# Both heads of a pair turned by DMA transposes in a two-layer attention kernel

## The chip, the cores and the metric

The kernel runs on one core of one Trainium2 chip. The metric is device time in microseconds of one execution. The median of three runs before the change is 2208.05 us (2207.29 to 2210.84). One further execution was recorded by the hardware profiler.

Engines are named as in the profile: PE is TensorE (matrix multiplication and transposes), DVE is VectorE, ACT is ScalarE, POOL is GpSimd, and SP is the queue that issues all transfers (DMA).

## The reference, cut to what matters

Two layers stand one behind the other. Each computes `x + W_out(attention(RMSNorm(x)) * silu(gate))`, with q, k, v and gate from one combined projection and an RMS norm per head on q and k. There are 2048 prompt rows and 64 sample rows, 1024 features and 16 heads of 64.

- Layer A: 16 query heads share 2 key heads; a query sees its own chunk of 64 rows and the 2 before; each head has a learned sink and a relative bias.
- Layer B: 16 query heads and 16 key heads; a query sees its own chunk and the 8 before; each head has a learned bias by clipped distance. No sinks.

```python
s = jnp.einsum('bqkgd,bskd->bkgqs', qg, k) * (dh ** -0.5) + bias
p = jax.nn.softmax(s, axis=-1)                     # layer B
o = jnp.einsum('bkgqs,bskd->bqkgd', p, v)
y = x + (o * jax.nn.silu(gate)) @ w_out
```

The softmaxed p comes out of the first product with queries on partitions, while the second product needs keys on partitions. So p has to be transposed, tile by tile. This transposition is the subject here.

## The kernel before, in words

**Precision.** Numbers are carried as two halves, a high and a low part. A projection is three matmuls per block of 128 features: high by high, high by low, low by high (L679 to L681). In layer B both halves are fp16, and powers of two (`S_W`, `C_B`, `G_B`) computed from the largest weight of each pair keep them in range.

**Work in layer B.** The 16 heads form 8 pairs (`hp`, 0 to 7). For each pair there are nine units: eight of 256 prompt rows (`u` 0 to 7, two tiles of 128 rows each) and one of the 64 sample rows, which stands between units 6 and 7. A unit is first projected (`gen`, `project`) and later attended.

**Two streams on PE.** PE's order is written out by hand. `pipeline` walks through the attention of the units; between its parts it calls `filler.to(mark)`, which emits as much of the projection work of later units (and, at the end, of the output projection) as a count of PE cost asks for. The other engines' orders come from a scheduler that simulates the program, so an instruction of SP, ACT, DVE or POOL can be placed earlier than it was written.

**A step.** A prompt unit has four steps, in the order (tile 0, head 0), (tile 1, head 0), (tile 0, head 1), (tile 1, head 1); a sample unit has one. A step does `scores`: the score matmuls into a PSUM tile `sb` (two such tiles exist), the biased minimum on DVE (L1420), the exponential on ACT (L1429). Then comes background work, filler, `due(step)` with everything promised for this step, and filler again. After the second step of a unit, `queries` of the next unit transposes q and k on PE into the only `tp` tile (PSUM).

**How p is turned.** `TURNED` lists the heads of a pair that go by DMA, in pairs 1 to 7.

- Head 0 (in `TURNED`): DVE adds log(2^14) to the minimum (L1425), `parts` copies p to fp16 on ACT (L1463) and has POOL subtract for the low half (L1464), both into one of three buffers named `values`; one step later `turn_p` issues the DMA transpose into a `pt` buffer (L1472; there are two). The products (`turned_products`, L1568) follow four steps after the second tile.
- Head 1 (not in `TURNED`): one step later `values` transposes p on PE, block by block, into an `sb` tile (L844), and `split_to` evicts it in two halves by ACT (L816) and DVE (L817). The products (`products`, L1607) follow three steps after the second tile. The transposes of the gates of the unit share the last of these `sb` tiles.
- Pair 0 and the sample unit always go by PE.

Both heads' products add into one PSUM tile `o` (there is one), which `finish` evicts, multiplies by the gates and stores.

**Background work.** `bg` is a list of small jobs: splitting weights (L467, L470), squares and scales of the q and k norms (L756 to L774), gates (L782, L783), low halves of queries (L1367, L1371). `bg.share` takes some from the list. In layer B it is called after every `scores` and after every `values`, so six times in a unit of pairs 1 to 7.

**Weights and the scale chain.** The weights of the next pair are loaded raw (SP, L445) and split into a ring of 12 chunks, 8 of which a pair uses. Four chunks are asked for three filler jobs ahead, the rest one job ahead. Their scale needs a chain: `input_across` (a transpose on PE of one column, L197, then DVE) and `input_scales` (a matmul, L212, then DVE, L213). `scale_work` calls them inside the projection of unit 5. Both use the `tp` tile.

Of the kernel before, what the change touches and what calls it, by code (L numbers as in the profile page):

```python
# [17 lines left out]
P = 128  # L18
# [6 lines left out]
NU = SEQ // UT  # L25
# [9 lines left out]
WB = 3  # L35
XB = 4
XN = 7
EARLY = 3
MORE = 4.7
WN = 12  # L40
AVG_A = 5.02
# [7 lines left out]
QY = 1  # L49
# [1 line left out]
HB, WB_, PB, VB = 2.0 ** 10, 2.0 ** 14, 2.0 ** 14, 16.0  # L51
LAG = 4
HALF = 5 * 2 * P
TURNED = (0,)

@with_exitstack
def hybrid_encoder_kernel(
# [34 lines left out]
    sb = ctx.enter_context(tc.tile_pool(name="sb", bufs=2))  # L92
# [163 lines left out]
    def scale_work(hp, u, e):  # L256
        at = 2 * u + e
        if hp < 7:
            if at < 8:
                scan(8 * (hp + 1) + at)  # L260
            elif at == 8:
                scan()
                input_top(hp + 1)
            elif at == 10:
                input_across(hp + 1)
            elif at == 11:
                input_scales(hp + 1)
            i = 64 + 3 * hp + (at - 11)
            if 11 <= at < 14 and i < 84:
                scan(i)  # L270
            elif at == 14:
                scan()
        elif u == 0:
            (output_top, output_across)[e]()
        elif at == 2:
            output_scales()
# [585 lines left out]
        return Q2[turn[0] % 2]  # L862


    class Filler:
        def __init__(self):
            self.jobs, self.n, self.gen, self.done, self.total = [], -1, None, 0.0, 0.0
            self.attending = False

        def add(self, prefetch, weights, gen, early=True):  # L870
            j = Item()
            j.prefetch, j.weights, j.gen, j.early = prefetch, weights, gen, early
            self.jobs.append(j)

        def step(self):
            if self.gen is None:
                self.n += 1
                if self.n >= len(self.jobs):
                    return False
                if self.n == 0:  # L880
                    self.x = self.jobs[0].prefetch()
                    self.jobs[0].weights()
                for q in self.x.items:
                    bg.run(q)
                if self.n + 1 < len(self.jobs):
                    nxt = self.jobs[self.n + 1]
                    self.x = nxt.prefetch()
                    if nxt.weights is not None:
                        nxt.weights()
                if self.n + EARLY < len(self.jobs):  # L890
                    nxt = self.jobs[self.n + EARLY]
                    if nxt.weights is not None and nxt.early:
                        nxt.weights(WN - 8)
                self.gen = self.jobs[self.n].gen()
# [16 lines left out]
    def layer_a():  # L911
# [4 lines left out]
        def add_unit(qd, place, unit):  # L916
# [117 lines left out]
                mine[0].mark = filler.total  # L1034
            if qd == 0 and unit is order[-1]:
                mine[0].mark += 8 * 3 * 256 / 2400
            filler.add(prefetch, weights if place == 0 else None, first if qd == 0 and u == 0 else gen, qd > 1)

        for qd in range(4):
            for place, unit in enumerate(order[2:5] + order[:2] + order[5:] if qd == 1 else order):  # L1040
# [215 lines left out]
    def layer_b():  # L1256
# [4 lines left out]
        def add_unit(hp, unit):  # L1261
# [14 lines left out]
                return x  # L1276

            def weights(*m):
                if hp not in st.emit:
                    (st.w[hp],), _, st.emit[hp] = load_weights(1, (w_in_b[hp], 512), scale=gsb[:, hp])  # L1280
                st.emit[hp](*m)
# [39 lines left out]

            filler.total += 8 * (6 if T == UT else 2) * 512 / 2400
            it.mark = filler.total
            filler.add(prefetch, weights if u == 0 else None, gen)

        for hp in range(8):
            for unit in order:
# [148 lines left out]
        def values(it, i, h, short):  # L1476
            u, T, tiles = it.unit
            tt, t0, n = tiles[i]
            if i == 0:
                it.ph[h], it.pl[h] = (  # L1480
                    t(x, [P, 5, 256], 2, F32R if u == NU else F16) for x in ("ph", "pl")
                )
            if u == NU:
                n, m, kb = P, 3, 0
            else:
                kt0 = max(tt - 4, 0)
                m, kb = tt - kt0 + 1, kt0 - it.base
            PT = psum_b("sb", 1024, 2)
            PTv = PT.rearrange("p (c x) -> p c x", x=P)
            gates_too = u != NU and it.hp > 0 and (i, h) == (1, 1)  # L1490
            for c in range(m):
                transpose(PTv[:, (kb + c) % 5, :n], it.p[i, h][:n, c * P : (c + 1) * P])
                if short:
                    short.pop(0)()
            while short:
                short.pop(0)()
            if gates_too:
                GT = PT[:, 5 * P : 5 * P + T]
                for e, (_, g0, _) in enumerate(tiles):
                    transpose(GT[:, g0 : g0 + n], it.G[:n, e * P : (e + 1) * P])  # L1500
            bg.anchor(*split_to(
                it.ph[h][:, :m, t0 : t0 + n], it.pl[h][:, :m, t0 : t0 + n], PTv[:, :m, :n],
                None if u == NU else PB,
            ))
            if gates_too:
                it.gt = gate_t(GT.rearrange("p (j s) -> p j s", j=1), T, G_B(it.hp))

        def then(it, i, h):
            late = it.hp > 0 and len(TURNED)
# [66 lines left out]
        def gates(it):  # L1576
            u, T, tiles = it.unit
            n = tiles[0][2]
            GT = psum("tp", 512, 1)
            for e, (_, t0, _) in enumerate(tiles):  # L1580
                transpose(GT[:, t0 : t0 + n], it.G[:n, e * P : (e + 1) * P])
            it.gt = gate_t(GT[:, :T].rearrange("p (j s) -> p j s", j=1), T, G_B(it.hp))
# [12 lines left out]
        def products(it, h):  # L1595
# [17 lines left out]
                product(short[0], 0)  # L1613

            def rest():
                if h == 1 and it.hp == 0:
                    gates(it)
                for y, x in enumerate(full):
                    if y:
                        product(x, 0)  # L1620
                    product(x, 1, stop=y == last)
                if h == 1:
                    finish(it)
# [11 lines left out]
        def pipeline():  # L1635
# [12 lines left out]
            def due(at):  # L1648
                flush()
                now = [x for x in todo if x[0] <= at]  # L1650
                todo[:] = [x for x in todo if x[0] > at]
                short, rests, vals = [], [], []
                for _, kind, x in now:
                    if kind == "products":
                        between, rest = products(*x)
                        short += between
                        rests.append(rest)
                    else:
                        {"values": vals, "call": rests}[kind].append(x)
                for x in vals:  # L1660
                    values(*x, short)
                    bg.share(BL, BP_, KC)
                for fn in short + rests:
                    fn()

            for x, it in enumerate(its):
# [13 lines left out]
                for y, (i, h) in enumerate(heads):  # L1680
# [6 lines left out]
                    if sample and x + 1 < len(its):  # L1687
                        queries(its[x + 1])
                        flush()
                        near = 1e9  # L1690
                    goal(2 * y + 2)
                    if not sample and y == QY and x + 1 < len(its):
                        queries(its[x + 1])
                        near = 1e9
# [234 lines left out]
```

## Time and profile before

| What | Value |
|---|---|
| median of three runs | 2208.05 us |
| profiled execution | 2212.35 us |
| its span | 2210.5 us |
| mean granted PE clock | 0.987 |
| PE, DVE, ACT, POOL busy | 95%, 70%, 64%, 45% of the span |
| DMA queue of SP | 58.0% of 16 engines' time |

In rows of groups, the last two numbers before the bar are the busy time in us and the mean duration of one in ns; after the bar stands the idle time of the engine just before them, and what ended it. A PE duration includes the latency of its pipeline, so it is longer than the distance to the next one. In rows of waits stand the total in us, how often, and the longest. In rows of the timeline stand start and duration in us. In rows of windows stand the stretch, its length, the busy time of PE, PEld (weight loads), DVE, ACT and POOL with the number of instructions in brackets, the granted PE clock, the DMA engines' busy share and GB/s. In the view of one line stand the shortest, median and longest duration in ns.

### The profile page before, as it was taken

What the parts mean: (1) busy time and instruction counts of PE and PEld (TensorE: products, weight loads), DVE (VectorE), ACT (ScalarE), POOL (GpSimd) and SP (SyncE); (2) the same over time, 40 slices, a digit from 0 to 9 for tenths busy, and PEclk for the clock granted to TensorE, in tenths of its full rate; (3) what the DMA queues carried; (4) which work ended last, traced back from release to release, by engine and by line L of the source; (5) the groups of instructions that cost most, each with busy time, mean ns of one, the idle gap of its engine ahead of it and who ended that gap; (6) DMA issues with size and microseconds to landing.
All of it is one profiled execution on the core that took longest, in us unless ns stands there. A gap on an engine that the chain in (4) does not pass through costs nothing.

```text
span 2210.5 us, 41329 instructions
## 1 busy us (share of the span) xinstructions
PE 2110.9 (95%) x13441; PEld 1526.6 (69%) x13441; DVE 1547.2 (70%) x4105; ACT 1424.8 (64%) x3610; POOL 999.5 (45%) x1509
## 2 busy tenths in 40 slices
PE   7999999999999999999999989999999999998999
PEld 6877888787889997555555555555555555566888
DVE  6769777677676456787777776777767767577542
ACT  6878878677785333666666766766667667576420
POOL 5645544334355355853444444444444445443000
PEclk9999999999999999999999999999999999999999
DMA  8856546856545667445465565664646556345664
GB/s 276 275 160 215 180 125 220 229 164 182 180 128 178 216 192 256 158 143 172 117 180 136 128 178 133 160 167 115 196 118 162 158 118 171 95 105 136 198 202 124
DMA packets 383096, 372.87 MB, mean 169 GB/s; under 512 B 174672, under 2 KB 320352, under 8 KB 382848
## 3 DMA queue, kind: packets, MB, share of 16 engines
q1 hardware_dynamic: 382880, 370.23, 58.0%
q8 instruction: 106, 1.74, 0.3%
q14 instruction: 110, 0.90, 0.1%
HBM read 257.59 MB, written 73.43 MB: 150 GB/s over the span
## 4 chain that ended last, share of the span: by engine, by line
PE 58%; DVE 15%; DMA 9%; ACT 8%; issue 6%; POOL 4%; SPq 1%; POOLq 0%; ACTq 0%; DVEq 0%
PE pj L679 9%; PE pj L681 9%; PE pj L680 9%; PE pj L1772 4%; PE pj L1774 4%; PE pj L1773 4%; DMA scan<-in_w_in_b_dram 3%; DVE p L1420 3%; PE sb L844 2%; PE sa L844 2%; PE o L1607 2%; PE tp L844 2%; PE o L1568 2%; PE sb L1416 1%; ACT p L1429 1%
## 5 line engine op out<-in xcount | busy, mean ns | idle before, releaser
L679 PE MATMUL pj<-wh,xx 128*128 128x512 f16 (+2 forms) x1648 | 644.6, 391 | 5.2 <-ACT pb L702 3.9
L681 PE MATMUL pj<-wh,xx 128*128 128x512 f16 (+2 forms) x1648 | 626.4, 380 | 2.5 <-POOL xx L564 2.5
L680 PE MATMUL pj<-wh,xx 128*128 128x512 f16 x1024 | 392.0, 383 | 0.0
L1429 ACT ACTIVATE p<-p,nm 128x640 f32<-128x640 f32 (+5 forms) x264 | 199.2, 754 | 202.6 <-DVE nm L1420 102.4
L1772 PE MATMUL pj<-xx,wh 128*128 128x264 f32 (+1 forms) x1024 | 291.4, 285 | 8.0 <-DVE res L1778 2.7
L1773 PE MATMUL pj<-xx,wh 128*128 128x264 f32 (+1 forms) x1024 | 288.8, 282 | 0.0
L680 PE MATMUL pj<-wl,xx 128*128 128x512 f32 (+1 forms) x624 | 234.1, 375 | 2.2 <-DVE wl L470 2.2
L1420 DVE CUSTOM_DVE_ANT_0 p<-sb,BT 128x640 f32<-128x640 f32 (+5 forms) x272 | 195.7, 720 | 44.7 <-PE sb L1417 42.3
L564 POOL TENSOR_TENSOR xx<-xraw,xx 128x528 fp32r<-128x528 f32 (+4 forms) x144 | 183.8, 1295 | 88.9 <-ACT xx L563 82.1
L1464 POOL TENSOR_TENSOR values<-p,values 128x640 f16<-128x640 f32 (+2 forms) x112 | 141.2, 1261 | 159.4 <-ACT values L1463 158.8
L1250 POOL TENSOR_TENSOR o<-gt,o 128x256 f32<-128x256 f32 (+1 forms) x132 | 100.8, 763 | 207.7 <-DVE o L1249 96.8
L761 POOL TENSOR_TENSOR f<-f,mhalf 128x4 f32<-128x4 f32 (+2 forms) x187 | 187.5, 1003 | 13.7
L681 PEld LDWEIGHTS <-xx 128*128 128x128 f16 x1024 | 101.0, 99 | 126.4 <-issue 4.7
L756 POOL TENSOR_TENSOR sq<-pa 128x256 f32<-128x256 f32 (+2 forms) x187 | 113.1, 605 | 147.1 <-ACT pa L715 94.3
L1156 ACT ACTIVATE p<-p,nm 128x257 f32<-128x257 f32 (+2 forms) x272 | 134.3, 497 | 51.1 <-DVE nm L1150 42.9
L774 DVE TENSOR_TENSOR pa<-pa,f 128x256 f32<-128x256 f32 (+3 forms) x221 | 120.3, 544 | 57.9 <-POOL f L761 53.2
L679 PEld LDWEIGHTS <-xx 128*128 128x128 f16 x1024 | 101.3, 99 | 71.9 <-issue 3.1
L680 PEld LDWEIGHTS <-xx 128*128 128x128 f16 x1024 | 101.1, 99 | 70.1 <-issue 3.0
L1774 PE MATMUL pj<-xx,wl 128*128 128x264 f32 x512 | 145.7, 285 | 0.8 <-DVE wl L463 0.8
L1774 PE MATMUL pj<-xx,wh 128*128 128x264 f16 x512 | 142.7, 279 | 2.1 <-DVE wh L460 2.1
L1150 DVE CUSTOM_DVE_ANT_0 p<-sa,BT,nsink 128x256 f32<-128x256 f32 (+2 forms) x272 | 117.4, 467 | 36.0 <-PE sa L844 29.9
L679 PEld LDWEIGHTS pj<-wh,xx 128*128 128x128 f32 x624 | 118.7, 190 | 23.0 <-ACT pb L702 4.8
(273 smaller groups left out, 5276.9 us busy)
## 6 DMA issues: line engine op xcount, KB each, us to landing
xx<-xsb SPq DMA_DIRECT2D x112, 512.0 KB, 4.1
xx<-xsa SPq DMA_DIRECT2D x88, 512.0 KB, 4.8
xraw<-oga SPq DMA_DIRECT2D x64, 264.0 KB, 3.6
xraw<-ogb SPq DMA_DIRECT2D x64, 264.0 KB, 3.7
xsa<-xx SPq DMA_DIRECT2D x32, 512.0 KB, 4.1
scan<-in_w_in_b_dram SPq DMA_DIRECT2D x64, 256.0 KB, 4.5
wl<-in_w_in_b_dram SPq DMA_DIRECT2D x64, 256.0 KB, 4.1
xraw<-in_x_dram SPq DMA_DIRECT2D x40, 256.0 KB, 4.0
```

Of the source, the lines that this page charges most:

```text
L564: nc.gpsimd.tensor_tensor(lo, rv, wide(hi), op=ALU.subtract)
L679: nc.tensor.matmul(ps[:n, :C], xh, wh, start=k == 0, stop=False)
L680: nc.tensor.matmul(ps[:n, :C], xh, wl, start=False, stop=False)
L681: nc.tensor.matmul(ps[:n, :C], xl, wh, start=False, stop=k == KC - 1)
L761: nc.gpsimd.tensor_tensor(fv, fv, mhalf[:n, :H], op=ALU.pow)
L1156: ex = nc.scalar.activation(pv[:n, h % 2, : nk + 1], pv[:n, h % 2, : nk + 1], AF.Exp, scale=-1.0, bias=nm[:n, h : h + 1], accum_out=sm[:n, ...
L1420: mi = nc.vector.tensor_tensor_reduce(out=p[r, :nk], in0=S[r, o : o + nk], in1=b, op0=ALU.add, op1=ALU.min, scale=1.0, scalar=3e38, accum_ ...
L1429: ex = nc.scalar.activation(p[:n, :nk], p[:n, :nk], AF.Exp, scale=-1.0, bias=it.nm[:n, c : c + 1], accum_out=it.sm[:n, c : c + 1],)
L1464: lo = nc.gpsimd.tensor_tensor(two[:, :, 1, :], pv, two[:, :, 0, :], op=ALU.subtract)
L1772: nc.tensor.matmul(ps[:, :OT], wh, oh, start=k == 0, stop=False)
L1773: nc.tensor.matmul(ps[:, :OT], wh, ol, start=False, stop=False)
L1774: nc.tensor.matmul(ps[:, :OT], wl, oh, start=False, stop=k == KC - 1)
```

## The change

- `TURNED` becomes `(0, 1)`: head 1 of pairs 1 to 7 goes through `parts`, `turn_p` and `turned_products` like head 0. Its products follow four steps after the second tile, and the sample's products and output one step later than before. The multiplication of the reciprocal sums (L1440) falls away, as both heads now carry the same factor, and a factor in `input_across` answers for it.
- `gates` of pairs 1 to 7 takes an `sb` tile of its own, at the time of head 1's products.
- `bg.share` in `due` is called at every step but the first, whether there are `values` or not: eight times a unit.
- `scale_work` puts the two links of the scale chain on a list; `pipeline` takes one link off after the last filler of a prompt unit's fourth step; `weights` of layer B takes what is still there. The second link is put there one tile later than it was called before.
- Four chunks of the next pair's weights are asked for two filler jobs ahead in layer B (`early` is 2), not three. Elsewhere this stays as it was.

```diff
-TURNED = (0,)
+TURNED = (0, 1)
...
             elif at == 10:
-                input_across(hp + 1)
-            elif at == 11:
-                input_scales(hp + 1)
+                held["chain"].append(lambda: input_across(hp + 1))
+            elif at == 12:
+                held["chain"].append(lambda: input_scales(hp + 1))
...
-                if self.n + EARLY < len(self.jobs):
-                    nxt = self.jobs[self.n + EARLY]
-                    if nxt.weights is not None and nxt.early:
+                for nxt in self.jobs[self.n + 2 : self.n + 4]:
+                    if nxt.weights is not None and nxt is self.jobs[min(self.n + nxt.early, len(self.jobs) - 1)]:
                         nxt.weights(WN - 8)
...
             def weights(*m):
+                while held["chain"]:
+                    held["chain"].pop(0)()
...
-            filler.add(prefetch, weights if u == 0 else None, gen)
+            filler.add(prefetch, weights if u == 0 else None, gen, 2)
...
-            gates_too = u != NU and it.hp > 0 and (i, h) == (1, 1)
...
-            if gates_too:
-                GT = PT[:, 5 * P : 5 * P + T]
-                for e, (_, g0, _) in enumerate(tiles):
-                    transpose(GT[:, g0 : g0 + n], it.G[:n, e * P : (e + 1) * P])
...
-            if gates_too:
-                it.gt = gate_t(GT.rearrange("p (j s) -> p j s", j=1), T, G_B(it.hp))
...
-            GT = psum("tp", 512, 1)
+            GT = psum_b("sb", 1024, 2) if it.hp and len(TURNED) else psum("tp", 512, 1)
...
-                if h == 1 and it.hp == 0:
+                if h == 1:
                     gates(it)
...
                 for x in vals:
                     values(*x, short)
+                if at:
                     bg.share(BL, BP_, KC)
...
                     goal(2 * y + 2)
+                    if not sample and y == QY + 2 and held["chain"]:
+                        held["chain"].pop(0)()
```

More of the change, by code (lines that the diff above doesn't have):

```diff
@@ L37 @@
 XN = 7
-EARLY = 3
 MORE = 4.7
@@ L862, in low_queries @@
         return Q2[turn[0] % 2]
+    held["chain"] = []
     class Filler:
@@ L868, in __init__, with add @@
             self.attending = False
-        def add(self, prefetch, weights, gen, early=True):
+        def add(self, prefetch, weights, gen, early=3):
             j = Item()
@@ L1036, in add_unit @@
                 mine[0].mark += 8 * 3 * 256 / 2400
-            filler.add(prefetch, weights if place == 0 else None, first if qd == 0 and u == 0 else gen, qd > 1)
+            filler.add(prefetch, weights if place == 0 else None, first if qd == 0 and u == 0 else gen, 3 * (qd > 1))
         for qd in range(4):
```

## The prediction

> **What bounds the kernel now.** First the page's head, then busy time in windows of one pair of heads (141.2 us is the distance at which the scan loads recur in the chain of work that ended last).
>
> ```profile
> span 2210.5 us, 41329 instructions
> PE 2110.9 (95%) x13441; PEld 1526.6 (69%) x13441; DVE 1547.2 (70%) x4105; ACT 1424.8 (64%) x3610; POOL 999.5 (45%) x1509
> ...
> core 0: us, PE busy (x) PEld busy (x) DVE busy (x) ACT busy (x) POOL busy (x), PEclk, DMA share, GB/s
> 1135.30:1276.50 141.20, 134.28 (x828) 80.07 (x828) 105.33 (x281) 96.08 (x243) 68.10 (x105) 1.00 0.57 149
> 1276.50:1417.70 141.20, 134.04 (x817) 79.73 (x816) 102.41 (x276) 95.34 (x242) 65.57 (x99) 0.99 0.56 149
> ```
>
> In layer B, where the whole change lies, TensorE works 134 of 141 us per pair; VectorE, its nearest rival, 102 to 105. So TensorE's own instructions are the bound, and 7 us a pair are waits. The view of waits of TensorE from 1058 to 2010 us (pairs 1 to 7) says which:
>
> ```profile
> PE sb L844 <- DVE nm L1420: 13.6, 6, 2.7
> PE tp L197 <- DVE KB L1371: 6.7, 6, 3.8
> PE sb L1416 <- DVE nm L1420: 5.6, 6, 1.9
> PE sb L844 <- ACT p L1429: 5.5, 5, 1.4
> PE sb L844 <- DVE pl L817: 3.7, 8, 0.9
> PE sb L1416 <- ACT gt L1237: 2.9, 3, 1.1
> PE sb L844 <- ACT values L719: 2.3, 1, 2.3
> ...
> PE tp L844 <- DVE scl L213: 1.3, 5, 0.3
> ```
>
> 25.1 us (13.6 + 5.5 + 3.7 + 2.3) stand in front of TensorE's transposes of the second head's p, 8.5 us (5.6 + 2.9) in front of score matmuls that share the two `sb` tiles with them, 8.0 us (6.7 + 1.3) at the scale chain. No row names `pt`: the DMA-transposed head is never waited for.
>
> **The change, part by part.**
>
> *Transposes leave TensorE.* A head of one pair has tiles of 1, 2, 3, 4 and twelve times 5 key blocks, 70 in all; seven pairs make 490 instructions. The first row's count agrees: 490, with 140 of pair 0 and 24 of the sample, is 654. The time of one is read from starts in the timeline, since its 0.27 us are latency:
>
> ```profile
> L844 PE MATMUL sb<-ident,p x654: 272/273/422, 899.5 to 2054.2; 128*128 128x128 f32 x164
> ...
> 1478.18 0.71 PE L844 MATMUL sb<-ident,p 128*128 128x128 f32 x5
> 1478.73 0.27 PE L844 MATMUL o<-ident,o 128*64 128x128 f32 x1
> ```
>
> Five take 0.55 us, 0.11 each: 490 x 0.11 = 54 us off the bound. The products stay as many, and the two gate transposes per unit only move to an `sb` tile of their own.
>
> *Waits in front of them.* The 25.1 us lose their instruction, and the score matmuls then find a free `sb` tile two steps back instead of one. But part of this wait is VectorE's debt at the end of a pair. Windows of 5 us and the worst wait there:
>
> ```profile
> 1291.50:1296.50 5.00, 3.41 (x18) 1.76 (x18) 4.70 (x13) 4.46 (x11) 2.07 (x4) 1.00 0.72 173
> 1296.50:1301.50 5.00, 2.33 (x10) 1.48 (x11) 5.00 (x11) 2.58 (x6) 2.66 (x5) 0.81 0.96 348
> ```
>
> VectorE is full there (4.70 and 5.00 of 5), TensorE waits, and its granted clock falls to 0.81. The scores will be late next in that place. Of 25.1 + 8.5 = 33.6 us I take 20 as gone; the ends are 0 and 34.
>
> *Scale chain.* Issued after the last step's filler instead of inside a projection, it finds its `tp` tile free; it can also fall together with the weights, when both links come at once. Of 8.0 us I take 5; ends 8 and -8, a loss as large as now.
>
> *What replaces the transposes.* Per tile, ACT and VectorE no longer split p out of PSUM (L816, L817); instead ACT copies it to fp16, POOL subtracts, SP issues a DMA transpose, and VectorE adds a constant to the minimum (L1425), while one small multiplication a unit (L1440) goes. Groups of pair 3's window, then views of single lines:
>
> ```profile
> L1464 POOL TENSOR_TENSOR values<-p,values 128x640 f16<-128x640 f32 (+4 forms) x16 | 20.0, 1251 | 23.4 <-ACT values L1463 23.3
> L817 DVE SCALAR_TENSOR_TENSOR pl<-sb,ph 128x640 f16<-128x640 f32 (+4 forms) x15 | 11.0, 730 | 2.0 <-ACT ph L816 1.9
> L1463 ACT CAST values<-p 128x640 f16<-128x640 f32 (+4 forms) x16 | 10.5, 653 | 0.2
> L816 ACT ACTIVATE ph<-sb 128x640 f16<-128x640 f32 (+4 forms) x16 | 10.0, 627 | 3.7 <-PE sb L844 3.5
> ...
> L1425 DVE TENSOR_SCALAR nm<-nm x112: 131/145/155, 1057.3 to 2041.1; 128x1 f32<-128x1 f32 x112
> L1440 DVE TENSOR_SCALAR sm<-sm x56: 160/169/259, 1068.7 to 2050.3; 128x2 f32<-128x2 f32 x56
> L1472 SPq DMA_TRANSPOSE pt<-values x112: 1184/1354/2478, 1058.8 to 2044.5; - x112
> DMA to landing us min/median/max: 2.3/3.5/7.5
> ```
>
> Per pair of now about 131 us: VectorE 102 - 16 x 0.73 + 16 x 0.145 - 8 x 0.17 = 92 (70%); ACT 95 - 10.0 + 10.5 = 96 (73%); POOL 66 + 20 = 86 (65%). None becomes the bound; they hide behind TensorE's 124 us. If that cover were gone POOL's 20 us a pair would be 140 us.
>
> *SP and the DMA engines.* 112 more issues of 1.35 us are 22 us a pair on SP's queue. A transfer's share of the engines is bounded by this stretch, which holds one transpose of ten 128x128 blocks and two 32 KB copies:
>
> ```profile
> 1519.52 1.33 SPq L1472 DMA_TRANSPOSE pt<-values  x1
> 1520.95 0.66 SPq L1360 DMA_DIRECT2D q<-q  x1
> ...
> 1520.00:1522.50 2.50, 2.50 (x15) 1.32 (x13) 1.87 (x5) 2.02 (x6) 1.27 (x3) 1.00 0.88 178
> 1522.50:1529.50 7.00, 6.54 (x41) 3.79 (x39) 5.72 (x22) 3.62 (x10) 2.99 (x6) 1.00 0.06 20
> ```
>
> 0.88 x 2.5 = 2.2 us at most, 35 us for 16: 0.56 x 141 = 79 becomes 114 of 131, 0.87. High, yet the next 7 us lie idle at 0.06, so transfers move rather than add up. Cover: from the issue of a head's last transpose to its products are three steps of 131 / 33 = 4.0 us, 12 us against 3.5 (worst 7.5). The ring of three `values` buffers comes round after three steps now, not six: POOL's 1.4 and the landing's 7.5 still fit. The `pt` buffer is freed by products in the step that wants it again, so a transpose can hold SP's queue for a fraction of a step; behind it stand xx loads, q copies and stores. I put nothing for this; ends 0 and 28 (4 us a pair at the full VectorE stretch).
>
> The Trainium skill, VectorE: DVE Perf Modes, section The three transpose paths, speaks against the change: it gives 1309 ns for a 128x128 block by DMA and prefers TensorE where PSUM will do. Ten blocks one by one would be 13.1 us, past the 12 us of cover, by some 1 us a unit, 60 us in all (an estimate from that page). The trace contradicts it: 3.5 us at the median.
>
> *POOL's order.* The query chain of the next unit runs over POOL (L756, L760, L761) and VectorE (L774) to transposes on TensorE. Its slack, in the tightest of six units of one pair, and what a colliding POOL instruction does to a VectorE one:
>
> ```profile
> 1688.47 0.42 DVE L774 TENSOR_TENSOR pa<-pa,f 128x256 f32<-128x256 f32 x1
> 1690.29 0.60 PE L844 MATMUL tp<-ident,pa 128*128 128x128 f32 x4
> ...
> 1498.10 0.91 POOL L1464 TENSOR_TENSOR values<-p,values 128x384 f16<-128x384 f32 x1
> 1498.24 0.93 DVE L783 SCALAR_TENSOR_TENSOR pb<-sq,pb 128x128 f32<-128x128 f32 x1 [0.19 <-ACT sq L782]
> ...
> L783 DVE SCALAR_TENSOR_TENSOR pb<-sq,pb x204: 215/410/1516, 35.4 to 2011.1; 128x128 f32<-128x128 f32 x64, 128x256 f32<-128x256 f32 x32, 128x64 f32<-128x64 f32 x4, 64x256 f32<-64x256 f32 x2
> ```
>
> 1.4 us of slack against one more subtraction of 1.25 us in front: mostly hidden. I take a loss of 5 us over all units; ends 0 and 118 (rival 1).
>
> *Edits with one answer.* The share at every step makes eight a unit instead of six and adds no instruction: 0, between -5 and 5. The first four weight chunks of a pair are split one job later; they run now at 1260 to 1269 us, and the ring lets the other four follow only from 1293:
>
> ```profile
> 1268.78 0.74 DVE L470 SCALAR_TENSOR_TENSOR wh<-wl,gsb,wh 128x512 f16<-128x512 f32 x1
> 1292.91 0.74 DVE L470 SCALAR_TENSOR_TENSOR wh<-wl,gsb,wh 128x512 f16<-128x512 f32 x1
> ```
>
> 24 us of room hide a shift of some 10; without it TensorE would wait four splits, 3 us a pair, 21. The second head's products come one step later, the sample's too; `o` is taken again two steps after that. Costs nothing but one more step at the end, covered by output projections.
>
> The sum: -54 - 20 - 5 + 5 = -74 us. The profiled execution took 2212.35 us (span 2210.5), 4.3 above the median of 2208.05; less 74 from each gives 2138 and 2134.
>
> **The rivals.**
>
> 1. *Slower: the query chain falls behind POOL.* If in each of 56 units two subtractions queue ahead of L760 or L761 (2.8 us) and a VectorE instruction is held 0.7 us more (0.93 against 0.22 for L783), 3.5 less the tightest slack of 1.4 is 2.1 us of wait a unit, 118 us instead of my 5. The sum is then +39: 2247. It decides from 79 / 56 = 1.4 us a unit. For it: rows above; against it: POOL stays idle a third of the time and the two subtractions come a step apart. The Trainium skill, SBUF — State Buffer, section SBUF: two separate sides, calls the port pair of VectorE and POOL an exclusive lock held for a whole instruction; the collision quoted agrees.
>
> 2. *Half given back.* VectorE's debt at the end of each pair and late transfers return the 20 us as score waits and add up to 28: -54 - 5 + 5 + (0 to 28), 2154 to 2182. For it: 5.00 of 5 us and a DMA share of 0.96 in the same window. Against: VectorE gives up 0.73 us a tile there.
>
> 3. *All gained.* All 34 and 8 us go and nothing comes: 2208 - 96 = 2112.
>
> 4. *The change doesn't do what it says.* Waits take up just what leaves, 2208: TensorE would have to be no bound, against 134 of 141 us.
>
> **How the numbers follow.** The forecast (2115 to 2153) 0.55; half back, up to 2203, 0.20; all gained 0.06; no change 0.04; slower 0.15. Within 0.2% (4.4 us) is about what a measurement of this kernel can't tell from no change. Faster 0.81, same 0.04, slower 0.15. The 8-in-10 range, 2105 to 2212, leaves out rival 1 and the lower end.
>
> **What the profile after would show.** Right: 164 or so `sb<-ident,p` transposes on TensorE; 224 DMA transposes; the waits at L844 and L1416 under 14 us; a pair in 130 to 132 us, TensorE 96% busy or more; POOL near 86. Wrong: rows of TensorE waiting at `tp` for L774 (rival 1), at the products for `pt`, at L1416 for L1420 over 30 us (rival 2), or ACT waiting at its copy for the transposes to land.

## The result, and the profile after

The change made the kernel about 1% slower: 2231.57 us (median, 2230.04 to 2233.74) against 2209.45 us (2207.29 to 2212.77) for the kernel before in the runs beside it, a ratio of 1.0095 with a 95% interval of 1.0079 to 1.0111. The forecast of 2134 us and its range, which ended at 2212, were wrong. Lines of the new kernel are numbered a little differently: L774 is now L773, L783 is L782, L470 is L469, L844 is L843; L1416 is now L1418, L1420 is L1422, L1464 is L1466, L1472 is L1474.

The head of the page after, and busy time in the middle 900 us of layer B, first of the kernel after and then of the kernel before:

```profile
span 2228.3 us, 40988 instructions
PE 2078.6 (93%) x12951; PEld 1477.0 (66%) x12951; DVE 1520.2 (68%) x4049; ACT 1436.8 (64%) x3610; POOL 1140.4 (51%) x1621
...
1100.00:2000.00 900.00, 806.72 (x4654) 453.50 (x4652) 617.66 (x1656) 600.49 (x1489) 535.60 (x722) 0.97 0.74 172
```

```profile
1100.00:2000.00 900.00, 860.62 (x5263) 512.37 (x5261) 661.49 (x1763) 613.34 (x1543) 428.75 (x649) 0.99 0.56 145
```

TensorE has 12951 instructions instead of 13441: exactly the 490 transposes are gone. Its busy time fell by 32.3 us (2110.9 to 2078.6), but the time in which it does nothing rose by 50.1 us, from 2210.5 - 2110.9 = 99.6 to 2228.3 - 2078.6 = 149.7. The difference, 17.8 us, is the growth of the span. So this is no story of a dearer instruction on TensorE. In the middle stretch it idles 93 us of 900 where it idled 39. No other engine is full there: VectorE works 618 of 900 us, POOL 536.

TensorE's waits between 1058 and 2040 us (total, times, longest) in the kernel after:

```profile
PE sb L1418 <- DVE nm L1422: 46.9, 26, 3.9
PE sb L1418 <- DMA q<-q: 12.7, 5, 4.3
PE o L843 <- POOL o L1528: 9.1, 6, 1.6
PE o L1521 <- ACT p L1431: 6.6, 5, 1.6
PE tp L196 <- DVE KB L1373: 6.2, 3, 5.5
PE sb L843 <- DVE nm L1422: 5.4, 5, 1.7
PE sb L1418 <- ACT gt L1237: 4.2, 7, 0.7
PE tp L211 <- DVE KB L1373: 4.2, 1, 4.2
```

The waits in front of the transposes went, and a larger one stands in front of the score matmuls. They need an `sb` tile that VectorE frees with its biased minimum (L1422, row `nm`); this cost 5.6 us before and costs 46.9 us now. Nothing waits for `pt`, and no row names `tp` and L773.

Why is VectorE late, when it works less than before? One place in the timeline (start, duration, instruction, in brackets the idle time before it):

```profile
1387.07 1.39 POOL L1466 TENSOR_TENSOR values<-p,values 128x640 f16<-128x640 f32 x1 [0.55 <-ACT values L1465]
1387.13 1.61 DVE L773 TENSOR_TENSOR pa<-pa,f 128x256 f32<-128x256 f32 x1
...
1388.77 0.82 DVE L1422 CUSTOM_DVE_ANT_0 p<-sb,BT 128x640 f32<-128x640 f32 x1
...
1389.66 0.32 PE L1418 MATMUL sb<-KA,q 128*128 128x384 f16 x1 [2.24 <-DVE nm L1422]
```

VectorE's L773 multiplies queries by their scale. It took 0.42 us in the row of the prediction. Here it starts just after a subtraction of POOL and ends just after it, 1.61 us long. The minimum of the softmax is the next instruction in VectorE's order and starts only then; TensorE waits 2.24 us for it, and 1.61 - 0.42 = 1.19 us of that is the stretched instruction. The wait is charged to L1422, which itself was not slow.

Over the whole execution, stretched instructions stand mainly in three groups of VectorE, all reading two inputs from SBUF: the query scales, the gates and the weight splits. Groups of VectorE, first before, then after (last numbers before the bar: busy us, mean ns):

```profile
L774 DVE TENSOR_TENSOR pa<-pa,f 128x256 f32<-128x256 f32 (+3 forms) x221 | 120.3, 544 | 57.9 <-POOL f L761 53.2 <-POOL f L769 2.5
L783 DVE SCALAR_TENSOR_TENSOR pb<-sq,pb 128x128 f32<-128x128 f32 (+3 forms) x204 | 97.7, 479 | 23.3 <-ACT sq L782 22.0
L470 DVE SCALAR_TENSOR_TENSOR wh<-wl,gsb,wh 128x512 f16<-128x512 f32 x64 | 60.0, 942 | 9.9 <-ACT wh L467 9.9
```

```profile
L773 DVE TENSOR_TENSOR pa<-pa,f 128x256 f32<-128x256 f32 (+3 forms) x221 | 150.4, 681 | 46.8 <-POOL f L760 42.2 <-POOL f L768 2.7
L782 DVE SCALAR_TENSOR_TENSOR pb<-sq,pb 128x128 f32<-128x128 f32 (+3 forms) x204 | 106.4, 522 | 40.1 <-ACT sq L781 38.5
L469 DVE SCALAR_TENSOR_TENSOR wh<-wl,gsb,wh 128x512 f16<-128x512 f32 x64 | 65.0, 1022 | 3.9 <-ACT wh L466 3.9
```

The same 489 instructions took 278.0 us before and 321.8 us after, 43.8 more. This sum, most of it ordinary working time, is called the held time below: no shape and no count changed, only what ran beside them. Taken one by one in pairs 1 to 7 (1058 to 2040 us), 96 of them last over 0.15 us longer than the shortest of their shape while a subtraction of POOL that had started first runs beside them: 84 us in all, 42 of it beside head 1's subtractions. In the kernel before it is 41 of them and 36 us.

### The profile page after: what moved, and what is told of

It reads as the page before. It is cut to its first block, busy times and chain, and to the rows that moved or that the text cites. A ratio compares the mean times of both kernels' runs of the same rounds, so it can differ in the third digit from the quotient of the medians.

```text
span 2228.3 us, 40988 instructions
## 1 busy us (share of the span) xinstructions
PE 2078.6 (93%) x12951; PEld 1477.0 (66%) x12951; DVE 1520.2 (68%) x4049; ACT 1436.8 (64%) x3610; POOL 1140.4 (51%) x1621
## 4 chain that ended last, share of the span: by engine, by line
PE 45%; DVE 21%; ACT 9%; DMA 9%; issue 8%; POOL 6%; SPq 1%; ACTq 0%; POOLq 0%; DVEq 0%
PE pj L678 7%; PE pj L680 7%; PE pj L679 7%; PE pj L1770 4%; PE pj L1772 4%; PE pj L1771 4%; DVE p L1422 4%; DVE pa L773 3%; DMA scan<-in_w_in_b_dram 3%; PE sa L843 2%; POOL values L1466 2%; DVE q L1369 2%; DVE o L1249 2%; ACT p L1431 2%; DMA scan<-in_w_o_b_dram 1%
## 5 line engine op out<-in xcount | busy, mean ns | idle before, releaser
L679 PE MATMUL pj<-wh,xx 128*128 128x512 f16 x1024 | 396.7, 387 | 0.9 <-DVE wh L469 0.9
L1466 POOL TENSOR_TENSOR values<-p,values 128x640 f16<-128x640 f32 (+2 forms) x224 | 281.5, 1257 | 133.7 <-ACT values L1465 131.2
L1422 DVE CUSTOM_DVE_ANT_0 p<-sb,BT 128x640 f32<-128x640 f32 (+5 forms) x272 | 195.9, 720 | 30.2 <-PE sb L1419 26.8
L773 DVE TENSOR_TENSOR pa<-pa,f 128x256 f32<-128x256 f32 (+3 forms) x221 | 150.4, 681 | 46.8 <-POOL f L760 42.2
L1465 ACT CAST values<-p 128x640 f16<-128x640 f32 (+2 forms) x224 | 147.1, 657 | 5.8
```

Of the source, the lines that this page charges most:

```text
L679: nc.tensor.matmul(ps[:n, :C], xh, wl, start=False, stop=False)
L773: nc.vector.tensor_tensor(sv, sv, fv.unsqueeze(2).to_broadcast([n, H, HD]), op=ALU.mult)
L1422: mi = nc.vector.tensor_tensor_reduce(out=p[r, :nk], in0=S[r, o : o + nk], in1=b, op0=ALU.add, op1=ALU.min, scale=1.0, scalar=3e38, accum_ ...
L1466: lo = nc.gpsimd.tensor_tensor(two[:, :, 1, :], pv, two[:, :, 0, :], op=ALU.subtract)
```

## The experiments

Three theories were put to the test. **S**: one of the scheduling edits (the share at every step, the late scale chain, the late weights) does the harm. **O**: the new order does it, above all the gates, which now take an `sb` tile in the middle of the scores. **P**: the 112 added subtractions of POOL hold VectorE. Each ratio is against the kernel before, run on the same chip.

### The parts one by one

The turned head alone, with the gates' own tile; share, chain and weights as before:

```diff
-TURNED = (0,)
+TURNED = (0, 1)
...
-            GT = psum("tp", 512, 1)
+            GT = psum_b("sb", 1024, 2) if it.hp and len(TURNED) else psum("tp", 512, 1)
```

> Only the turned head and the gates' own sb tile; share, scale chain and early weights as before. Theory S (the three scheduling edits cost the time, the turned head gains): 2150 us or less. Theory O (the softmax of VectorE comes late in its fixed order, and the gates' sb tile leaves the next unit's first scores only one step of room): 2225 to 2240, with more than 35 us of TensorE waiting for the biased minimum at the score matmuls. Theory P (112 more POOL subtractions hold VectorE): 2225 to 2240 too, with rows of a k-norm scale (mean 0.54 us before, 0.68 after) as long as after.

Measured: 2259.77 us, ratio 1.0224 (1.0197 to 1.0251), above every range expected. Its waits on TensorE, 1058 to 2040 us:

```profile
PE pj L679 <- ACT wh L467: 28.9, 12, 4.2
PE pj L680 <- DVE wh L470: 23.7, 18, 2.6
PE sb L1416 <- DVE nm L1420: 14.7, 11, 2.6
```

With one head fewer under `values`, the background work gets four shares a unit instead of six, and the weights come too late: 52.6 us. The held time is already 317.1 us here. The share at every step is thus no embellishment of the change; the turned head needs it.

The share alone, on the kernel before:

```diff
                 for x in vals:
                     values(*x, short)
+                if at:
                     bg.share(BL, BP_, KC)
```

> The kernel before with the share at every step alone. Theories O and P: within 5 us of before (2205 to 2213), since head 1 still goes by TensorE. Theory S: 2215 or more.

Measured: 2230.94 us, 1.0089 (1.0059 to 1.0119). This is theory S's range. Background work earlier on VectorE is probably work ahead of the softmax: the score wait for L1420 rises from 5.6 to 15.5 us, and the transposes wait longer for VectorE's eviction (3.7 us before). But two waits for POOL are new as well (8.7 us for the gates' factors, L1448, and 6.8 us for the gated output, L1533), and the transposes wait less for the minimum (3.9 us, 13.6 before), so no single wait explains the 19 us:

```profile
PE sb L1416 <- DVE nm L1420: 15.5, 22, 2.5
PE sb L844 <- DVE pl L817: 9.4, 14, 1.3
```

Held time 272.6 us, less than before, so this is another cause than P.

The chain and the weights' time alone, on the kernel before:

```diff
-                input_across(hp + 1)
+                held["chain"].append(lambda: input_across(hp + 1))
...
-            filler.add(prefetch, weights if u == 0 else None, gen)
+            filler.add(prefetch, weights if u == 0 else None, gen, 2)
...
+                    if not sample and y == QY + 2 and held["chain"]:
+                        held["chain"].pop(0)()
```

> The kernel before with the scale chain at the last step and the early weights two jobs ahead alone. Theories O and P: 2200 to 2210, a few us less for the 8 us of waits at the tp tile. Theory S: 2215 or more, by waits for weights or for the chain.

Measured: 2207.71 us, 0.9983 (0.9969 to 0.9997), 4 us in the direction forecast, though the chain's wait at L197 is still 6.7 us, so it isn't shown that the chain brought them. The three parts give +48, +19 and -4 us alone (medians against 2211.6) and +22 together (2231.57 against 2209.45): they don't add up, since the share repairs what the turned head breaks.

### POOL's subtraction

The kernel after, with the subtraction for head 1 left out (its low half is not computed, and the three buffers are zeroed once; everything else stands):

```diff
+                    nc.gpsimd.memset(held["two"].rearrange("p a b c -> p (a b c)").bitcast(F32), 0.0)
...
-            lo = nc.gpsimd.tensor_tensor(two[:, :, 1, :], pv, two[:, :, 0, :], op=ALU.subtract)
+            if h == 0:
+                lo = nc.gpsimd.tensor_tensor(two[:, :, 1, :], pv, two[:, :, 0, :], op=ALU.subtract)
```

> The kernel after without POOL's 112 subtractions for head 1: the low half of its p is not computed (stale values stand in its place), everything else is issued as before. Theory P: the 30 us that the k-norm scales lost on VectorE come back, the score matmuls' wait falls under 20 us, 2165 to 2190. Theory O: the tile still leaves one step of room; some of the lateness goes, 2205 to 2225.

Measured: 2175.69 us, 0.9822 (0.9795 to 0.9849). Page head and waits of TensorE (here L1419 and L1423 are the scores and their minimum):

```profile
span 2175.0 us, 40694 instructions
PE 2064.2 (95%) x12951; PEld 1473.3 (68%) x12951; DVE 1473.7 (68%) x4049; ACT 1433.0 (66%) x3610; POOL 1005.5 (46%) x1510
...
PE sb L1419 <- DVE nm L1423: 27.9, 21, 3.0
PE o L1523 <- ACT p L1432: 7.2, 5, 1.6
PE tp L196 <- DVE KB L1374: 4.1, 1, 4.1
PE sb L1419 <- DMA q<-q: 3.5, 5, 0.9
```

Every instruction of TensorE stands as in the kernel after (12951), and 53 us of span are gone: 39 us of idle time and 14 us of busy time, the latter with the granted clock, 0.979 in the kernel after and 0.986 here. Held time 272.4 us. The time is in theory P's range; the score wait, 27.9 us, did not fall under 20 as P had it. This shows that the subtraction costs the time, not yet how: POOL is also less busy and free earlier. Two memsets of the same half in place of each subtraction keep POOL busy without reading SBUF (the low half of head 1 is zero):

```diff
-            lo = nc.gpsimd.tensor_tensor(two[:, :, 1, :], pv, two[:, :, 0, :], op=ALU.subtract)
+            if h == 0:
+                nc.gpsimd.tensor_tensor(two[:, :, 1, :], pv, two[:, :, 0, :], op=ALU.subtract)
+            else:
+                for _ in range(2):
+                    behind(nc.gpsimd.memset(two[:, :, 1, :], 0.0).ins, hi.ins)
```

> The kernel after with each of POOL's 112 subtractions for head 1 replaced by two memsets of the same low half (so that half is zero and part of p's precision is left out): POOL stays about as busy, but no longer reads SBUF there. If POOL's queue is what costs (its own in-order lateness), the time stays at 2220 or more. If the collision of its reads with VectorE's two-input instructions costs, it falls to that of the run without the subtraction, 2170 to 2185, and the k-norm scale's mean falls from 0.76 to 0.55 us.

Measured: 2182.61 us, 0.9869 (0.9847 to 0.9892). Page head, the memsets among POOL's groups of 1100 to 2000 us, and TensorE's waits:

```profile
span 2181.0 us, 40961 instructions
PE 2063.0 (95%) x12951; PEld 1471.9 (67%) x12951; DVE 1479.6 (68%) x4049; ACT 1434.9 (66%) x3610; POOL 1114.9 (51%) x1733
...
1100.00:2000.00 900.00, 836.68 (x4967) 479.16 (x4966) 620.97 (x1759) 640.39 (x1583) 547.58 (x873) 0.98 0.78 182
...
L1470 POOL MEMSET values<- 128x640 f16 (+2 forms) x210 | 118.1, 571 | 2.3
...
PE sb L1418 <- DVE nm L1422: 25.2, 20, 3.0
PE sb L1418 <- DMA q<-q: 12.5, 6, 4.2
```

POOL works 548 of 900 us, more than the 536 of the kernel after, and the time is 49 us shorter. The three groups of VectorE are back at what they were before, 275.7 us together:

```profile
L773 DVE TENSOR_TENSOR pa<-pa,f 128x256 f32<-128x256 f32 (+3 forms) x221 | 123.4, 558 | 36.0 <-POOL f L760 31.1 <-POOL f L768 2.7
L782 DVE SCALAR_TENSOR_TENSOR pb<-sq,pb 128x128 f32<-128x128 f32 (+3 forms) x204 | 97.0, 476 | 42.8 <-ACT sq L781 41.2
L469 DVE SCALAR_TENSOR_TENSOR wh<-wl,gsb,wh 128x512 f16<-128x512 f32 x64 | 55.3, 882 | 3.7 <-ACT wh L466 3.6
```

The memsets do not wait for ACT's copy in POOL's queue as the subtraction does (`behind` fixes their place in the written order only). So that wait was put back, by a copy of one element ahead of the two memsets (the low half of head 1 is again not computed):

```diff
+                nc.gpsimd.tensor_copy(two[:, 0, 1, 0:1], two[:, 0, 0, 0:1])
+                for _ in range(2):
+                    nc.gpsimd.memset(two[:, :, 1, :], 0.0)
```

> As the run with two memsets in place of each of head 1's subtractions on POOL, but ahead of them POOL copies one element of ACT's fp16 copy, so that POOL waits for ACT in its order as the subtraction does, and reads almost nothing. Left out as there: the low half of head 1's p is zero. If the subtraction's long read of SBUF beside VectorE's two-input instructions costs, the time stays at 2178 to 2192. If POOL's place in the order behind ACT costs, it returns to 2220 or more.

Measured: 2187.65 us, 0.9896 (0.9863 to 0.9929). That is 5 us from the memsets without the wait, with overlapping intervals, and 44 us from the kernel after: neither POOL's in-order wait nor its occupancy explains the loss. They may cost something: the two kernels with memsets lie 7 to 16 us above the one with nothing in the subtraction's place. A wait for the subtraction's result is no explanation either. In the kernel after, only POOL's own instructions wait for it among those of the computing engines (rows of L1466: us, times):

```profile
who waited for it (us, times):
  POOL ko L794: 1.4, 5
  POOL values L1466: 1.3, 1
```

What is left of the subtraction is that it reads SBUF for 1.26 us at a time. Held time 284.1 us, though L773 alone is still at 664 ns on average (681 in the kernel after): here head 0's subtractions stretch it. So a long L773 does not cost time as such; what it costs is shown at the end of this section.

The same subtraction on VectorE, which leaves the computation whole:

```diff
-            lo = nc.gpsimd.tensor_tensor(two[:, :, 1, :], pv, two[:, :, 0, :], op=ALU.subtract)
+            lo = (nc.gpsimd, nc.vector)[h].tensor_tensor(two[:, :, 1, :], pv, two[:, :, 0, :], op=ALU.subtract)
```

> The kernel after with head 1's low half subtracted on VectorE instead of POOL. VectorE gets back about as much work as it lost (112 times some 0.7 us). Theory P: no port collisions of the added kind, 2190 to 2215. Theory O: VectorE's queue is longer, the softmax later still, the wait of the score matmuls over 47 us, 2230 to 2260.

Measured: 2188.46 us, 0.9891 (0.9874 to 0.9909), faster than both kernels and 1.5 us below theory P's range. As nothing is left out here, the gain does not come of zeros in the low half. Page head, and the new group of VectorE in 1100 to 2000 us:

```profile
PE 2061.3 (94%) x12951; PEld 1470.6 (67%) x12951; DVE 1562.0 (72%) x4161; ACT 1438.0 (66%) x3610; POOL 1028.2 (47%) x1509
...
L1466 DVE TENSOR_TENSOR values<-p,values 128x640 f16<-128x640 f32 (+2 forms) x104 | 86.0, 826 | 3.3 <-ACT values L1465 2.4
```

VectorE, the engine that is late in the kernel after, gets 112 more instructions of 0.83 us and the kernel gains 43 us. So VectorE's load is not what costs here. Moving the query scale L773 to POOL on top brought nothing:

```diff
-            nc.vector.tensor_tensor(sv, sv, fv.unsqueeze(2).to_broadcast([n, H, HD]), op=ALU.mult)
+            (nc.vector, nc.gpsimd)[spread and bg.lazy and "VH" in held].tensor_tensor(
+                sv, sv, fv.unsqueeze(2).to_broadcast([n, H, HD]), op=ALU.mult
+            )
```

> Head 1's low half on VectorE, and layer B's scaling of q and k by their norm moved from VectorE to POOL, where its factor is made. That instruction was the one most often held (mean 0.70 us with the subtraction on VectorE, against 0.42 at the median) and VectorE also waited 25 us for its factor. Collision theory: 2165 to 2183. If POOL's queue then delays the queries, 2190 or more, with waits at the tp transposes for POOL.

Measured: 2188.81 us, 0.9899 (0.9867 to 0.9931), between the two ranges expected.

### The gates' place

The kernel after, with the gates' transposes in the `tp` tile instead of an `sb` tile:

```diff
-            GT = psum_b("sb", 1024, 2) if it.hp and len(TURNED) else psum("tp", 512, 1)
+            GT = psum("tp", 512, 1)
```

> The kernel after with the two gate transposes in the tp tile instead of an sb tile. Theory O: the first scores of a unit regain two steps of room; the wait of the score matmuls for the biased minimum falls from 47 us to under 20, and the time to 2190 to 2205. Theory P: the VectorE debt stays, 2225 to 2235.

Measured: 2263.10 us, 1.0231 (1.0206 to 1.0256), above both ranges expected. The score wait is gone and a worse one has come, since this tile is shared with the query transposes and the scale chain:

```profile
PE tp L843 <- DVE KB L1373: 46.1, 21, 3.8
PE tp L196 <- ACT gt L1237: 22.5, 6, 4.0
PE tp L843 <- ACT gt L1237: 20.7, 6, 4.0
```

The gates in the unused last 256 columns of the step's own score tile:

```diff
-            GT = psum_b("sb", 1024, 2) if it.hp and len(TURNED) else psum("tp", 512, 1)
+            GT = held["S"][:, 768:1024] if it.hp else psum("tp", 512, 1)
```

> The kernel after with the two gate transposes written into the unused last 256 columns of the score tile of the same step, so that no sb tile is taken for them and the next unit's first scores find a tile freed two steps back. Theory O (that tile left one step of room, and VectorE's softmax is later than one step): the 47 us of score matmuls waiting for the minimum fall under 15 and the 4 us behind the gates' eviction go; with the clock that idle time costs, 2170 to 2195. Theory P (POOL's subtractions make VectorE late and the lateness is paid somewhere anyway): 2215 to 2232, with the wait moved.

Measured: 2227.70 us, 1.0068 (1.0042 to 1.0093). The gates' transposes now wait for VectorE's minimum themselves (66.8 us at L843 for L1422), so the tile was not freed of the wait: the time is in theory P's range, and the run says little about O.

The gates in their own tile, but two steps earlier:

```diff
+                if last and h:
+                    todo.append((LAG - 2, "call", lambda: gates(it)))
...
-                gates(it)
```

> The kernel after with the gates' two transposes and their sb tile moved two steps earlier, from the fourth step of the next unit to its second, where VectorE is less behind. Nothing else changes. Theory O (the tile taken at the fourth step leaves the next scores one step of room, where softmax is latest): the 47 us of score matmuls waiting for the minimum fall under 20, 2185 to 2210. Theory P: the lateness is paid anyway, 2222 to 2235.

Measured: 2220.38 us, 1.0034 (1.002 to 1.0048), between the two ranges and 2 us from theory P's. The score wait halves, the one for the gates' eviction grows:

```profile
PE sb L1418 <- DVE nm L1422: 24.6, 18, 2.8
PE sb L1418 <- ACT gt L1237: 12.8, 8, 2.0
```

Place matters for 11 to 13 us (medians, and ratios). With the subtraction on VectorE as well nothing of that is left:

```diff
+                if last and h:
+                    todo.append((LAG - 2, "call", lambda: gates(it)))
...
+            lo = (nc.gpsimd, nc.vector)[h].tensor_tensor(two[:, :, 1, :], pv, two[:, :, 0, :], op=ALU.subtract)
```

> Both: head 1's low half on VectorE, and the gates two steps earlier. If both conditions cost time on their own, 2160 to 2180. If the subtraction was all, 2184 to 2192 as with it alone.

Measured: 2189.49 us, 0.9889 (0.986 to 0.9918), as with the subtraction on VectorE alone.

### Six shares or eight

The share cost 19 us on the kernel before, so it was cut to six a unit in the kernel after, and in the one with the subtraction on VectorE:

```diff
-                if at:
+                if at and y in (0, 3):
                     bg.share(BL, BP_, KC)
```

> The kernel after with the share in due only at the first and the fourth step, where the kernel before had it by its values: six shares a unit instead of eight. If the two added shares cost time here as they did alone on the kernel before (20 us), 2205 to 2215. If a unit without PE-transposed head needs them (weights come late, as in the run with the turned head alone), 2235 to 2260, with waits of projections for split weights.

> The same six shares, with head 1's low half subtracted on VectorE. If the added shares cost 20 us beside the collisions, 2165 to 2175, which would be the fastest. If they are needed, 2190 to 2215.

Measured: 2222.28 us, 1.0045 (1.0026 to 1.0063), and 2195.72 us, 0.9931 (0.9905 to 0.9957): 9 to 11 us better in the one, which is between the two ranges expected, and 7 to 9 worse in the other, where the intervals just touch. So two of the eight shares cost 9 to 11 us beside POOL's subtractions, and nothing without them. With POOL subtracting, six lower the held time to 312.0 us; with VectorE subtracting they raise it to 291.8.

### All kernels with the full change, side by side

| Kernel | Held time, us | Time, us |
|---|---|---|
| after | 321.8 | 2231.57 |
| gates in the score tile | 319.0 | 2227.70 |
| gates two steps earlier | 315.2 | 2220.38 |
| six shares | 312.0 | 2222.28 |
| subtraction on VectorE, six shares | 291.8 | 2195.72 |
| subtraction on VectorE | 284.8 | 2188.46 |
| memsets that wait | 284.1 | 2187.65 |
| subtraction on VectorE, gates earlier | 280.4 | 2189.49 |
| memsets | 275.7 | 2182.61 |
| no subtraction | 272.4 | 2175.69 |

From the last to the first row 49 us of held time go with 56 us of time. But the rows form two groups, with POOL subtracting for head 1 and without, and within a group the order is loose (the gates two steps earlier have more held time than six shares, and less time). So the sum marks the kernels with the subtraction; it is not a price in itself. The kernel with the gates in `tp` (313.6 us, 2263.10) has a wait of its own.

What a stretched instruction costs can be read from the traces one wait at a time. For each wait of TensorE for the minimum in pairs 1 to 7, VectorE was followed back from the minimum as long as it had no pause of more than 0.1 us, and the stretch (over 0.15 us above the shortest of the same shape) of every scale, gate or weight split found there was counted once, up to the length of the wait:

| Kernel | L773, mean ns | Waits for the minimum, us (times) | Behind a stretched instruction, us (times) |
|---|---|---|---|
| before | 544 | 19.2 (12) | 8.6 (11) |
| after | 681 | 52.3 (31) | 19.3 (23) |
| memsets that wait | 664 | 31.3 (24) | 3.8 (7) |
| subtraction on VectorE | 650 | 36.2 (34) | 5.7 (8) |
| memsets | 558 | 25.2 (20) | 2.6 (4) |
| no subtraction | 565 | 28.6 (22) | 2.1 (3) |

In the kernel after, all 19.3 us stand behind L773. With the memsets that wait, and with the subtraction on VectorE, L773 is nearly as long, but seldom just ahead of a minimum that TensorE waits for. So the collision costs where it falls in VectorE's order. Against the four kernels without the subtraction on POOL, the kernel after loses 27 to 39 us of idle time on TensorE and 13 to 17 us of busy time, the latter at a lower granted clock; 14 to 17 us of the idle time are the difference in the last column. The rest of it was not followed from instruction to instruction.

## Why the prediction was wrong

**The transposes, -54 us: right in kind and near in size.** Instruction count and `pt` came as forecast: 112 more DMA transposes, landing in 3.5 us at the median as before (the kernel after; duration of the issue, and landing):

```profile
L1474 SPq DMA_TRANSPOSE pt<-values x224: 1180/1348/3281, 1055.3 to 2071.1; - x112
...
DMA to landing us min/median/max: 2.3/3.5/8.7
```

With memsets in place of the subtraction TensorE's busy time fell by 2110.9 - 2063.0 = 47.9 us. In the kernel after it fell by 32.3 only. An estimate: the granted clock went from 0.987 to 0.979, and 0.8% of 2079 us is 17 us. Why it fell is not shown: with the gates two steps earlier TensorE idles as long (149.0 us, here 149.7), and the clock is 0.985.

**POOL's order, +5 us: this is the step that failed.** It should have been 44 to 60 us (the ratios of the four kernels without that subtraction on POOL, 0.9822 to 0.9896, against 1.0095). The prediction had the right row: L783 at 0.93 us beside a subtraction (instead of 0.26, the shortest 128x128 one in the trace before; the 0.22 that it took is of a 128x64 one). But it priced the collision at one place alone, the query chain, whose slack of 1.4 us hides it, and rival 1 asked for waits at `tp`. None came. What VectorE does late in an in-order queue is whatever stands behind the stretched instruction, and here that is the minimum that frees the scores' tile. The term should have been bounded by what can be held: 112 reads of 1.26 us are 141 us, of which 43.8 us came true as held time, and then by the waits that can stand behind it. That 43.8 us of held time lie near the 44 us of loss proves little: only 19.3 us of stretch, beside either head's subtractions, stand just ahead of a wait for the minimum. Rival 1 was right about the held instruction and about the sign, wrong about the place.

The Trainium skill, SBUF — State Buffer, section SBUF: two separate sides, says that a VectorE instruction with two SBUF inputs contends only with a GpSimd instruction that reads SBUF. The runs agree: the memsets, which only write, left the three groups at 275.7 us, the reading subtraction took them to 321.8. It also says that whichever starts first takes the ports for the whole instruction; in the place shown the subtraction started 0.06 us earlier, and L773 ended 0.28 us after it.

**Waits in front of the transposes, -20 us: wrong also without the collision.** The rows counted there, at L844 and L1416, stood at 33.6 us before. After, they are 46.9 + 5.4 + 4.2 = 56.5 us (the prediction's own bound was 14). Without the subtraction they are still 27.9 us and two small rows: about what they were. The prediction left 13.6 of the 33.6 us for "the scores will be late next"; it was nearly all of it. This is rival 2 with its sign, L1416 waiting for L1420 over 30 us in the kernel after, and its times, 2154 to 2182, are close to those of the kernels without the subtraction on POOL, 2176 to 2188.

**Scale chain, -5 us: nothing.** 8.0 us before, 6.2 + 4.2 = 10.4 after, 7.5 without the subtraction (4.1 at L196 and 3.4 at L211).

**SP and the DMA engines, 0 with an end of 28:** the scores' wait for the `q` copies rose from 0.4 us (a row of the kernel before, below) to 12.7, and is 0.2 to 12.5 us in the four kernels without the subtraction on POOL. For the kernel after, 0 was too low, though its ends held it.

```profile
PE sb L1416 <- DMA q<-q: 0.4, 1, 0.4
```

**One step later for the sample, "costs nothing": wrong.** Waits at the `o` tile are 9.1 + 6.6 us and a row of 1.6 after, no row before, and 10.4 us without the subtraction (7.2, 2.4 and 0.8). The sample's products (L1521) now come just when the output of unit 6 is being taken out of the only `o` tile (the row names ACT's exponential, but VectorE's L1249, which reads that output, ends within 0.03 us of it, as at 1340.96 us), and their transposition (L843) is reached before POOL has multiplied by the gates (L1528).

**Edits with one answer.** The weights, right: TensorE waits 0.9 us for them in the kernel after. The share, "0, between -5 and 5": 19 us on the kernel before, where it was tried alone; in the changed kernel two of the eight cost 9 to 11 us beside the subtraction and nothing without it.

The sum: the forecast was -74 us of span, the measurement +17.8, 92 us apart. With the memsets or without the subtraction the span is 29.5 or 35.5 us below that of the kernel before: so 47 to 53 us of the 92 go with the subtraction on POOL, 5 of which the prediction had, and some 44 to 50 us are gains that the other terms promised and didn't bring: 6 to 7 us of TensorE's busy time, and 36 to 43 us of idle time that was to fall by 25 and rose by 11 to 18.

What stays open: why the scores wait 25 to 35 us for VectorE's minimum even without the subtraction on POOL. VectorE is at 621 to 698 of 900 us there, so its order is suspected, but no run moved the softmax ahead of the background work. Open too is what lowers the clock in the kernel after.

## What to carry to other kernels

Price an instruction moved to POOL by what it does to VectorE as well: list VectorE's instructions with two SBUF inputs, count how often POOL's SBUF reads can meet them, and ask what stands behind them in VectorE's order. A wait charged to an instruction of normal length is a hint to look at the instruction ahead of it. When a bound engine loses work, count the waits that stood in front of that work as kept until you can name what makes the late engine earlier.

## What was not expected of the hardware

- Giving the busier of two engines more work made the kernel faster: 112 subtractions took 1.26 us each on POOL and 0.83 us on VectorE, and the kernel with them on VectorE was 43 us faster.
- Two memsets of POOL (0.57 us each) beside VectorE's two-input instructions left their length alone; one subtraction of 1.26 us stretched the one shown by 1.19 us.
- TensorE's mean granted clock does not follow its idle time alone: it is 0.979 in the kernel after and 0.985 with the gates two steps earlier, with 149.7 and 149.0 us of idle time; with the gates in `tp` it is 0.968, with 171.1 us.
- A stretched instruction need not cost anything: L773 took 681 ns on average in the kernel after and 664 ns with the memsets that wait, which is 44 us faster.
